# An order between the dense stream and the mixers, and a new allotment of dense work to each mixer step

## The chip, the cores and the metric

The kernel runs on one core of a Trainium2 chip. The metric is the device time of one execution in microseconds (us). Before the change three executions took 3931.73, 3942.15 and 3942.74 us; the median is 3942.15 us. A profile was taken of one execution, which took 3931.44 us.

## The reference

One layer of a hybrid encoder, for a prompt of 2048 rows and a sample group of 8 streams with 16 new rows each (128 rows). Model width 1024, four mixers A, B, C, D with four heads of 64, feed-forward width 2816, all in f32:

```python
h = rms_norm(x, norm_mix_g) * (1 + sc1) + sh1
cols = h @ w_in                          # columns for A, B, C, D
oa = gdn_mixer(cols_A, ...)              # A: gated delta rule in chunks of 64, state carried from chunk to chunk
ob = stick_breaking_attend(qb, kb, vb)   # B: strictly causal
oc = forgetting_attend(qc, kc, vc, f)    # C: causal softmax with a forget bias
od = band_attend(qd, kd, vd, bias)       # D: own chunk and the 8 before it
mixed = concat([oa] + [rms_norm(o, mg[i]) for i, o in enumerate((ob, oc, od))])
x = x + ga1 * (mixed @ w_o)
h = rms_norm(x, norm_ffn_g) * (1 + sc2) + sh2
u = causal_depthwise_conv(h @ w_up, ffn_conv_w, state)   # width 3
a, b = split(u)
x = x + ga2 * ((silu(a) * b) @ w_down)
```

The sample rows go through the same layer with caches of 1024 past rows (512 for D) and a carried state for A and for both convolutions. All new caches and states are outputs too.

## The kernel before

**Two streams of work.** The program is traced from two Python generators. The *dense* stream does the matrix products with the large weights: first the projections `proj` for four parts of 512 prompt rows (part 0 with the 128 sample rows), then four feed-forward blocks `ffn0` to `ffn3`, one a part (block 3 with the sample rows), each with the product by `w_o` at its start, `w_up` with the convolution, and `w_down`. Each f32 operand is split into a high and a low half (`hh`/`hl`, `mh`/`ml`, `gh`/`gl`), and three products with the halves (high by high, low by high, high by low) make one f32 product. The weights come through rings of tiles (`wu`, `wd`) that are loaded from a copy in DRAM. Between two feed-forward blocks stands a changeover: the next part's rows of `mixed` (the mixers' results, which went to DRAM) and of x are loaded to tiles `raw` and turned on PE, and the finished sums `acc` are turned and stored.

The *mixer* stream runs, part by part: for part 0, B, then A as `local0` (all of A that needs no state) and `steps0` (the recurrence), then C and D; for part 1, B1, C1, D1, then the sample rows of B (`sB`) side by side with `local1` and then `steps1`; for parts 2 and 3, the sample rows of C (D) side by side with `local2`, `steps2` (`local3`, `steps3`), then B, C and D of that part. `attn_prompt` writes a part's result of B, C or D with stores `mixed<-nsq` (line 874), and loads its operands from DRAM at the head of each phase: `qT` (line 902), the bias `add` (911), `kT` (997) and `vhl` (1004).

**What sets the order.** `weave` (line 133) alternates between the two. It takes one step of the mixers, under a priority so much higher (offset 100000) that the scheduler, which lays out each engine's instruction order ahead of time, places a mixer's instruction as soon as it takes it to be ready; each mixer step yields a number, its *pace*, which is added to a debt, and then dense steps are taken until the debt is paid (each says what it is worth). The pace comes from `lab` (line 167), which looks the phase's name up in the table `PACE` by its first two letters, then by its first. So `B2` and `C3` have entries of their own, `D` stands for D0 to D3, `lo` for local0 to local3, `st` for steps0 to steps3, and `s` for the sample phases. A phase with a low pace leaves dense work for later. Where the two streams depend on each other they yield a mark in place of a number: `mixers` waits for `proj0` to `proj3`, a feed-forward block for the mark `mix0` to `mix3` of its part. When the mixers are through, the dense stream goes on alone: this is most of `ffn3`.

`Order.step` (line 91) is taken around each step of either stream. It keeps the last PE instruction of every mixer step in the list `mix`. A dense step whose list `mix` is longer than `lag` gets an order dependency for its first PE instruction, on the last one of the mixer step `lag + 1` entries back. The dependency is one for the scheduler only (NoSync: both are on PE, no semaphore comes of it). `LAG` is 1000 (line 2131).

**PSUM.** Four pools of banks: `d` (3) for the dense products and turns, `z` (2), `ptr` (2) and `oT` (1) for the mixers. All matmuls are issued on line 89 and all transposes on line 92, so the tile's name tells what an instruction is: `d` for the dense stream, `z`, `ptr`, `oT` for the mixers.

Of the kernel before, what the change touches and what calls it, by code (L numbers as in the profile page):

```python
# [16 lines left out]
D = 1024  # L17
# [58 lines left out]
class Order:  # L76
# [17 lines left out]
    def step(self, g, dense, lag):  # L94


        self.now = []
        self.K.small = self.K.smalls[int(dense)]
        try:
            return next(g)  # L100
        finally:
            if not dense:
                if self.now:
                    self.mix.append(self.now[-1])
            elif self.now and len(self.mix) > lag:
                self.tc.add_manual_dep(self.now[0].ins, self.mix[-1 - lag].ins.name,
                                       mybir.DependencyInfo(mybir.DependencyClass.NoSync, mybir.DependencyReason.DATA), reason="order")
            self.now = None
# [17 lines left out]
def weave(K, dense, mixers, ahead, lag):  # L126

    debt, block = 0.0, None  # L130
    live = True

    def run_dense():
        nonlocal block, live
        try:
            c = K.pe.step(dense, True, lag)
        except StopIteration:
            live = False
            return 0.0
        block = c if isinstance(c, str) else None  # L140
        return 0.0 if block else c

    while True:
        try:
            with K.tc.high_priority(offset=ahead):
                c = K.pe.step(mixers, False, lag)
        except StopIteration:
            break
        if isinstance(c, str):
            while c not in K.done:  # L150
                run_dense()
                assert live and (block is None or block in K.done)
            continue
        debt += c
        while debt > 0 and live and (block is None or block in K.done):
            debt -= run_dense()
        debt = min(debt, 0.0)
    while live:
        run_dense()
# [6 lines left out]

def lab(nc, name, g):

    pace = PACE.get(name[:2], PACE.get(name[:1]))
    num = lambda: int(nc.get_next_instruction_name().split("-")[1]) if DEBUG else 0  # L170
    k = 0
    while True:
        a = num()
        try:
            c = next(g)
        except StopIteration as e:
            if DEBUG:
                MARKS.append((a, num(), name))
                print("phase", name, "steps", k)
            return e.value  # L180
        k += 1
        if DEBUG:
            MARKS.append((a, num(), name))
        yield pace * PHI if pace and not isinstance(c, str) else c


PACE = {"ga": 0.3, "B0": 0.9, "B1": 1.1, "B2": 0.8, "B3": 0.65, "C0": 0.8, "C1": 0.75, "C2": 0.6, "C3": 0.6, "D": 0.8, "lo": 0.6, "st": 0.6, "s": 0.4}


def chain(*gens):  # L190
    for g in gens:
        yield from g
# [232 lines left out]
def proj_stage(K, parts):  # L425
    yield from lab(K.nc, "proj", proj_parts(K, parts))
# [1051 lines left out]
def attn_samples(K, g, beside):  # L1478

    A = Ctx()  # L1480
    A.ev, A.wb, A.pb, A.sb = Eng(K.nc, 0.5), 2, 2, 1
    A.psum = lambda: K.mps("ptr")
    A.w = lambda m: A.sp.tile([P, P], F32, name="wn", bufs=1) if m <= P else A.sp.tile([P, 512], F32, name="w", bufs=A.wb)
    with K.tc.tile_pool(name="s" + g, bufs=1, side="right", reuse_waits="tile") as A.sp:
        yield from merge((lab(K.nc, "s" + g, samples_steps(K, A, g)), 1.0), (beside, 1.0))
# [260 lines left out]
def feed_stage(K):  # L1746

    tc = K.tc
    F = [Feed(K, p) for p in range(4)]
    yield "mix0"  # L1750
    copies = [(c, b) for c in "kv" for b in range(NB)]
    with ExitStack() as last:
        with tc.tile_pool(name="ff", bufs=2, side="left", reuse_waits="tile") as sp:
            for p in range(3):
                if p == 0:
                    rows = [sp.tile([P, 512], F32, name="acc", bufs=KT) for _ in range(KT)]
                    mod_columns(K, sp, rows)
                    yield from F[0].mixed(sp, raws(sp, F[0]))
                    yield from F[0].residual(0, sp, raws(sp, F[0]))
                    yield from F[0].residual(1, sp, raws(sp, F[0]))  # L1760
                if p < 2:
                    sa = lambda: sp
                else:
                    sa = lambda: last.enter_context(tc.tile_pool(name="fa", bufs=2, side="right", reuse_waits="tile"))
                sa = yield from lab(K.nc, f"ffn{p}", feed_block(K, F[p], sp, sp, F[p + 1], sa, copies))
        with tc.tile_pool(name="ff3", bufs=2, side="left", reuse_waits="tile") as sp:
            yield from lab(K.nc, "ffn3", feed_block(K, F[3], sa, sp, None, None, copies))
# [260 lines left out]
def mixers(K, G, p):  # L2028


    nc, O, I = K.nc, K.O, K.I
    beside = lambda g, n, q: merge((g, n), (lab(nc, f"gates{q}", gates(K, q)), 15))
    B = lab(nc, f"B{p}", attn_prompt(K, "B", p))
    local = lab(nc, f"local{p}", G.local_all(p))
    rest = lambda: chain(*[lab(nc, f"{g}{p}", attn_prompt(K, g, p)) for g in "CD"])
    if p < 3:
        local = beside(local, 50, (0, 2, 3)[p])
    rule = chain(local, lab(nc, f"steps{p}", G.steps_all(p)))

    def samples():  # L2040
        yield "proj3"
        if p == 3:
            nc.sync.dma_start(out=O["gdn_conv_p"], in_=K.a_pre[SEQ - 3:SEQ, 0:768])
        G.beside(True)
        yield from attn_samples(K, "BCD"[p - 1], rule)
        G.beside(False)

    yield f"proj{p}"
    if p == 0:
        yield from B  # L2050
        nc.sync.dma_start(out=O["gdn_conv_s"], in_=K.a_pre[SEQ:].rearrange("(b s) c -> b s c", s=16)[:, 13:16, 0:768])
        for _ in chain(gate_stage(K, NP, NT), gate_stage(K, 0, 4)):
            pass
        yield from rule
        yield from rest()
    elif p == 1:
        yield from beside(B, 79, 1)
        yield from rest()
        yield from samples()
    else:  # L2060
        yield from samples()
        yield from B
        yield from rest()
    K.done.add(f"mix{p}")


def trunk(tc, I, O):
# [3 lines left out]
    with ExitStack() as st:  # L2071
# [38 lines left out]
        dense = chain(proj_stage(K, parts), feed_stage(K))  # L2110
        K.pe.step(dense, True, LAG)
        with tc.issue_after(K.anchor.ins):
            load_consts(K, cp)
        gate_tiles(K, cp)
        G = Gdn(K, cp)
        weave(K, dense, chain(*[mixers(K, G, p) for p in range(4)]), 100000, LAG)

# [10 lines left out]


NF = 22  # L2130
LAG = 1000
OUTS = [
    ("y_p", (SEQ, D), (1, SEQ, D)), ("y_s", (P, D), (NB, 16, D)),
    ("gdn_conv_p", (3, 768), (1, 1, 3, 768)), ("gdn_state_p", (4, 64, 64), (1, 1, 4, 64, 64)),
# [26 lines left out]
```

## Time and profile before

| | before |
|---|---|
| runs, median (lowest to highest) | 3942.15 us (3931.73 to 3942.74) |
| profiled execution | 3931.44 us, span 3929.7 us |
| mean granted clock of TensorE | 0.961 |
| PE busy | 3660.0 us (93%), 22763 instructions |
| weight loads busy (beside PE) | 3162.0 us (80%) |
| VectorE (DVE) busy | 2437.6 us (62%) |
| ScalarE (ACT) busy | 1536.7 us (39%) |
| GpSimd (POOL) busy | 1431.8 us (36%) |
| HBM | 213 GB/s over the span |

An engine's busy time is the union of its instructions; PE's overlap, so a busy PE is not one at its peak, and the printed duration of a matmul is longer than the distance from one start to the next. The granted clock is the share of the full TensorE clock that the throttle allows. A window's row gives, for each engine, busy time and number of instructions, then the clock, the share of time in which the 16 DMA engines move data, and GB/s. In waits, `z L89 <- DMA kT<-kTD` reads: an instruction of line 89 that writes `z` waited for the transfer into `kT`.

### The profile page before, as it was taken

Reading aid. Unit: us, or ns where it says so; the run is one execution under the profiler, and the core shown is the slowest. Engines: PE = TensorE matmul, PEld = TensorE weight load, DVE = VectorE, ACT = ScalarE, POOL = GpSimd, SP = SyncE. Lnnn points to the kernel's source line nnn. Section 1 sums busy time; section 2 is a strip of 40 time slices with the busy share of each in tenths; the row PEclk is TensorE's granted clock in tenths of the full one; section 3 lists DMA queues with packets and bytes.
Section 4 is the critical chain, followed back from the end, with each engine's and each line's share of the span. In section 5 each row is a group of like instructions: output and inputs, shape, how many; then the busy total and the mean of one; then the engine's idle time right before and its main releaser. Section 6 shows DMA issues by size and latency. Waiting matters only on the chain. (4 is left out here: it accounts for less than half of the span.)

```text
span 3929.7 us, 66233 instructions
## 1 busy us (share of the span) xinstructions
PE 3660.0 (93%) x22763; PEld 3162.0 (80%) x22763; DVE 2437.6 (62%) x5592; ACT 1536.7 (39%) x3353; POOL 1431.8 (36%) x3487
## 2 busy tenths in 40 slices
PE   6998999999998999998999999689999996899999
PEld 4987889989986677775888788468787875899999
DVE  5668655464567785775487566765776665344444
ACT  4455323353355533542254344323553444232121
POOL 4456244362434434441465112333553112121121
PEclk7999999999999999998999999899999997999999
DMA  7887968777687888887454646564544633544442
GB/s 226 285 279 242 305 205 296 274 268 250 227 267 239 295 292 289 286 291 237 150 195 144 224 156 210 166 195 164 190 146 164 180 121 123 202 141 142 152 142 93
DMA packets 529077, 830.37 MB, mean 211 GB/s; under 512 B 112651, under 2 KB 351259, under 8 KB 528476
## 3 DMA queue, kind: packets, MB, share of 16 engines
q1 hardware_dynamic: 527269, 825.16, 63.4%
q8 instruction: 181, 2.97, 0.3%
q0 software_dynamic: 1472, 0.97, 0.1%
q14 instruction: 155, 1.27, 0.1%
HBM read 611.81 MB, written 224.16 MB: 213 GB/s over the span
## 5 line engine op out<-in xcount | busy, mean ns | idle before, releaser
L89 PE MATMUL d<-hh,wu 128*128 128x512 f32 (+1 forms) x3520 | 1016.8, 365 | 6.7 <-DMA wu<-keptw_up 4.5
L89 PEld LDWEIGHTS d<-hh,wu 128*128 128x128 f32 x3520 | 633.0, 190 | 98.7 <-issue 8.5
L89 PE MATMUL d<-w,hh 128*128 128x256 f32 (+2 forms) x3536 | 684.6, 289 | 26.3 <-DVE w L458 9.3
L89 PE MATMUL d<-hl,wu 128*128 128x512 f32 (+1 forms) x1760 | 639.3, 363 | 0.9 <-DVE hl L1862 0.7
L89 PEld LDWEIGHTS d<-w,hh 128*128 128x128 f32 x3536 | 562.2, 193 | 44.2 <-DVE w L458 11.6
L89 PE MATMUL d<-gh,wd 128*128 128x512 f32 (+1 forms) x1760 | 530.9, 370 | 13.0 <-DVE acc L1822 10.4
L89 PE MATMUL d<-w,hl 128*128 128x256 f32 (+2 forms) x1768 | 504.7, 287 | 0.2 <-DVE hl L407 0.2
L1912 DVE SCALAR_TENSOR_TENSOR cv<-u,fcw,cv 128x512 f32<-128x512 f32 (+1 forms) x440 | 299.9, 704 | 185.8 <-ACT cv L1910 177.7
L1822 DVE SCALAR_TENSOR_TENSOR acc<-d,mod,acc 128x512 f32<-128x512 f32 (+2 forms) x432 | 280.4, 655 | 187.7 <-PE d L89 187.1
L89 PEld LDWEIGHTS d<-gh,wd 128*128 128x128 f32 x1760 | 319.5, 190 | 67.2 <-DVE acc L1822 18.2
L89 PEld LDWEIGHTS d<-hl,wu 128*128 128x128 f32 x1760 | 333.3, 189 | 45.4 <-issue 3.7
L89 PEld LDWEIGHTS d<-w,hl 128*128 128x128 f32 x1768 | 338.8, 192 | 4.8 <-issue 3.3
L89 PE MATMUL d<-gl,wd 128*128 128x512 f32 (+1 forms) x880 | 319.7, 363 | 1.0 <-DVE gl L1974 1.0
L89 PE MATMUL z<-kT,qT 128*128 128x512 f32 (+3 forms) x864 | 261.2, 390 | 32.0 <-DVE mx L772 15.3
L839 ACT CAST wh<-ptr 128x512 fp32r<-128x512 f32 (+1 forms) x372 | 198.3, 552 | 208.6 <-PE ptr L92 116.8
L840 DVE TENSOR_TENSOR wl<-ptr,wh 128x512 fp32r<-128x512 f32 (+1 forms) x372 | 232.6, 639 | 74.7 <-ACT wh L839 68.7
L1899 ACT COPY u<-d 128x512 f32<-128x512 f32 (+1 forms) x220 | 110.3, 502 | 414.4 <-PE d L89 404.7
L740 DVE TENSOR_TENSOR_SCAN pr<-sn,pr,zeros 128x512 f32<-128x512 f32 (+3 forms) x172 | 223.8, 1308 | 31.4 <-ACT sn L732 24.6
L92 PE MATMUL ptr<-ident,w 128*128 128x128 f32 x1448 | 228.7, 278 | 13.5 <-POOL w L742 5.6
L1914 POOL COPY hal<-u 128x2 f32<-128x2 f32 x176 | 47.7, 271 | 523.2 <-ACT u L1899 520.9
L742 POOL TENSOR_TENSOR w<-w,pr 128x512 f32<-128x512 f32 (+3 forms) x168 | 187.6, 1119 | 114.2 <-DVE pr L740 61.2
L789 ACT ACTIVATE w<-w,nm 128x512 f32<-128x512 f32 (+3 forms) x284 | 174.2, 616 | 107.8 <-DVE nm L782 84.8
(610 smaller groups left out, 7175.1 us busy)
## 6 DMA issues: line engine op xcount, KB each, us to landing
wu<-keptw_up SPq DMA_DIRECT2D x264, 512.0 KB
w<-win SPq DMA_DIRECT2D x132, 512.0 KB
wd<-keptw_down SPq DMA_DIRECT2D x132, 512.0 KB
keptw_up<-wu SPq DMA_DIRECT2D x88, 512.0 KB
wu<-keptw_o SPq DMA_DIRECT2D x48, 512.0 KB
win<-w SPq DMA_DIRECT2D x44, 512.0 KB
raw<-in_w_up_dram SPq DMA_DIRECT2D x88, 256.0 KB
keptw_down<-wd SPq DMA_DIRECT2D x44, 512.0 KB
```

The costliest lines, as they stand in the source:

```text
L89: return self.note(self.nc.tensor.matmul(out, lhsT, rhs, **k))
L92: return self.note(self.nc.tensor.transpose(*a, **k))
L740: nc.vector.tensor_tensor_scan(out=pr[:, 0:m][:, ::-1], data0=sn[:, :m][:, ::-1], data1=K.zeros[:r, :m], initial=carry, op0=ALU.mult, op1= ...
L742: nc.gpsimd.tensor_tensor(w[:, :m], w[:, :m], pr[:, 1:m + 1], op=ALU.mult)
L789: self.K.nc.scalar.activation(w, w, AF.Exp, bias=self.nm, accum_out=self.l[:, s:s + 1])
L839: nc.scalar.copy(wh[:, c0:c1], pt[:, c0:c1])
L840: nc.vector.tensor_tensor(wl[:, c0:c1], pt[:, c0:c1], f(wh[:, c0:c1]), op=ALU.subtract)
L1822: nc.vector.scalar_tensor_tensor(acc[k][:, c0:m], ps[:, :m - c0], gate[:, k, 0:1], acc[k][:, c0:m], op0=ALU.mult, op1=ALU.add)
L1899: nc.scalar.copy(u[:, 2 + c0:2 + m], ps[:, :m - c0])
L1912: nc.vector.scalar_tensor_tensor(o, tap(i), cw[:, i:i + 1], o, op0=ALU.mult, op1=ALU.add)
L1914: nc.gpsimd.tensor_copy(K.hal[:, fi], tail)
```

## The change

Two things change. First, the order dependency holds only for dense steps that are traced after the projections' end (`proj3`) and before the mixers' end (`mix3`), and `LAG` is 12: there the first PE instruction of a dense step comes no earlier in PE's order than the last one of the mixer step 13 entries back. Second, the table of paces: a full name such as `local0` is looked up first, and the paces of B2, B3, C2, C3, D2, D3, of local1 to local3, steps1 to steps3 and of the sample phases are higher (D0, D1, local0 and steps0 keep theirs).

```diff
@@ Order.step
-            elif self.now and len(self.mix) > lag:
+            elif self.now and len(self.mix) > lag and "proj3" in self.K.done and "mix3" not in self.K.done:
                 self.tc.add_manual_dep(self.now[0].ins, self.mix[-1 - lag].ins.name,
@@ lab
-    pace = PACE.get(name[:2], PACE.get(name[:1]))
+    pace = PACE.get(name, PACE.get(name[:2], PACE.get(name[:1])))
...
-PACE = {"ga": 0.3, "B0": 0.9, "B1": 1.1, "B2": 0.8, "B3": 0.65, "C0": 0.8, "C1": 0.75, "C2": 0.6, "C3": 0.6, "D": 0.8, "lo": 0.6, "st": 0.6, "s": 0.4}
+PACE = {"ga": 0.3, "B0": 0.9, "B1": 1.1, "B2": 1.0, "B3": 0.83, "C0": 0.8, "C1": 0.75, "C2": 0.75, "C3": 0.75, "D0": 0.8, "D1": 0.8, "D": 0.9,
+        "local0": 0.6, "steps0": 0.6, "lo": 1.35, "st": 1.35, "s": 0.9}
...
-LAG = 1000
+LAG = 12
```

Both kernels have the same PE instructions; their order differs from the 4938th row of PE's on. Where the dense work stands is counted here, in PE's order, from the first mixer matmul of a phase to the first of the next (products of 512 columns or less into `d`, plus transposes into `d`; "others" are the mixers' own PE instructions). The times are those at which these first matmuls start in the trace of before, and the last row's time ends with the span's last products.

| phase | time before, us | dense before | others | dense after |
|---|---|---|---|---|
| D1 | 1085 to 1198 | 273 + 109 | 272 | 149 + 109 |
| sB, local1 | 1198 to 1464 | 727 + 0 | 513 | 594 + 0 |
| steps1 | 1464 to 1541 | 192 + 0 | 247 | 185 + 0 |
| sC, local2 | 1541 to 1852 | 736 + 96 | 673 | 884 + 0 |
| steps2 | 1852 to 1980 | 401 + 0 | 304 | 161 + 96 |
| B2 | 1980 to 2188 | 598 + 0 | 488 | 522 + 0 |
| C2 | 2188 to 2392 | 575 + 0 | 488 | 575 + 0 |
| D2 | 2392 to 2485 | 139 + 16 | 272 | 397 + 0 |
| sD, local3 | 2485 to 2637 | 250 + 80 | 376 | 360 + 96 |
| steps3 | 2637 to 2764 | 386 + 0 | 304 | 330 + 0 |
| B3 | 2764 to 3037 | 707 + 0 | 648 | 708 + 0 |
| C3 | 3037 to 3269 | 451 + 0 | 648 | 486 + 0 |
| D3 | 3269 to 3319 | 0 | 272 | 126 + 32 |
| changeover to ffn3 | 3319 to 3365 | 42 + 112 | 0 | 0 + 80 |
| ffn3 | 3365 to 3930 | 3576 + 40 | 88 | 3576 + 40 |

The order of PE's instructions at three places, as the scheduler left it. A row gives the line, the operation, out<-in, the tile's shape and how often it repeats. First, PE in steps2, before the change: a small product of the recurrence (`z<-Z,lT`, `oT<-kbv,lA`) among dense ones.

```order
L89 MATMUL d<-hh,wu 128x512 x2
L89 MATMUL z<-Z,lT 128x128 x4
L89 MATMUL d<-hl,wu 128x512
L89 MATMUL d<-hh,wu 128x512
L89 MATMUL d<-hl,wu 128x512
L89 MATMUL d<-hh,wu 128x512 x3
L89 MATMUL d<-hl,wu 128x512
L89 MATMUL d<-hh,wu 128x512 x2
L89 MATMUL d<-hl,wu 128x512
L89 MATMUL d<-hh,wu 128x512 x2
L89 MATMUL oT<-kbv,lA 128x64 x4
```

After the change the same pair of products, and those behind it, stand so:

```order
L89 MATMUL z<-Z,lT 128x128 x4
L89 MATMUL oT<-kbv,lA 128x64 x4
L92 MATMUL d<-ident,acc 128x128 x12
L89 MATMUL z<-lT,Z 128x128 x4
L89 MATMUL oT<-vn,kbv 128x128 x2
L89 MATMUL z<-S,gqet 128x128
L89 MATMUL z<-vn,lQ 128x64 x2
L89 MATMUL z<-S,gqet 128x128
L89 MATMUL z<-vn,lQ 128x64 x2
L92 MATMUL d<-ident,acc 128x128 x4
L89 MATMUL oT<-lA,lN 64x64 x4
```

Dense products stood between two dependent products of the recurrence; now there are fewer, and part of them are the transposes of `acc`, of the changeover from ffn0 to ffn1, which stood in local2 before.

Second, PE from C3 (its last rows are `oT<-wh,vhl` and the turn `oT<-j_676,os`) to D3 (whose scores are `z<-kT,qT`), before:

```order
L89 MATMUL oT<-wh,vhl 128x256
L89 MATMUL oT<-wl,vhl 128x256
L89 MATMUL oT<-j_676,os 128x64 x2
L89 MATMUL z<-kT,qT 128x512 x2
L89 MATMUL z<-kT,qT 128x384 x2
L89 MATMUL z<-kT,qT 128x128 x2
L89 MATMUL z<-kT,qT 128x256 x4
L89 MATMUL z<-kT,qT 128x128 x2
```

and after:

```order
L89 MATMUL d<-gh,wd 128x512 x2
L89 MATMUL d<-gl,wd 128x512
L89 MATMUL d<-gh,wd 128x512
L89 MATMUL oT<-j_676,os 128x64 x2
L89 MATMUL z<-kT,qT 128x512 x2
L89 MATMUL z<-kT,qT 128x384 x2
L89 MATMUL d<-gh,wd 128x512
L89 MATMUL d<-gl,wd 128x512
L89 MATMUL d<-gh,wd 128x512 x2
```

Dense products now stand ahead of C3's last turn and behind D3's second pair of scores, and none between the turn and the first scores, as before.

Third, SyncE's queue at the same place, which issues the stores and loads in its order, before:

```order
L874 DMA mixed<-nsq 128x4x64
L866 DMA hg<-in_merge_g_dram 128x64
L874 DMA mixed<-nsq 128x4x64
L902 DMA qT<-qTD 128x1024
L911 DMA add<-skew 128x640
L997 DMA kT<-kTD 128x512 x2
```

and after, where every line of the file is one further down:

```order
L875 DMA mixed<-nsq 128x4x64
L867 DMA hg<-in_merge_g_dram 128x64
L1801 DMA wu<-keptw_up 128x1024 x6
L875 DMA mixed<-nsq 128x4x64
L903 DMA qT<-qTD 128x1024
L912 DMA add<-skew 128x640
L998 DMA kT<-kTD 128x512 x2
```

Six loads of the dense stream's weights now stand ahead of C3's last store; D3's loads follow that store in both.

## Prediction

> **What bounds the kernel now.** I read the page's slices first, then the busy time of each stage, then the same stages with the tile `d` alone, and last the waits of the thin stages. The dense stream writes all its products to the PSUM tile `d`, the mixers write theirs to `z`, `ptr` and `oT`, so the count of `d` says how much dense work stands in a stage.
>
> ```profile
> PE   6998999999998999998999999689999996899999
> PEclk7999999999999999998999999899999997999999
> ```
>
> PE is at nine tenths or more nearly everywhere, so what can be won lies in a few slices: the head, which this change doesn't touch, the slices 25 and 26 (2456 to 2652 us) and 33 to 35 (about 3240 to 3440 us). First the price of a matmul where nothing waits: starts that follow each other in a run of dense products (start, us, what, count), a run of transposes, and a run of mixer products.
>
> ```profile
> 2599.66 0.62 PE L89 MATMUL d<-mh,wu 128*128 128x512 f32 x2
> 2600.12 0.39 PE L89 MATMUL d<-ml,wu 128*128 128x512 f32 x1
> 2600.34 0.62 PE L89 MATMUL d<-mh,wu 128*128 128x512 f32 x2
> ...
> 2448.01 0.71 PE L92 MATMUL d<-ident,raw 128*128 128x128 f32 x5
> 2448.55 0.49 PE L92 MATMUL ptr<-ident,w 128*128 128x128 f32 x3
> ```
>
> Three dense products start within 0.68 us, which makes 0.227 us each; five transposes take 0.54 us, 0.109 us each. The printed durations (0.62) overlap, so I do not use them. Now the stages: time, PE busy and count, PEld, DVE, ACT, POOL, granted clock, DMA share, GB/s.
>
> ```profile
> 1852.00:1980.00 128.00, 125.41 (x706) 103.53 (x706) 56.70 (x111) 33.08 (x61) 45.91 (x94) 1.00 0.51 172
> 1980.00:2188.00 208.00, 204.76 (x1090) 171.97 (x1089) 158.58 (x207) 101.76 (x204) 120.07 (x206) 1.00 0.49 167
> 2188.00:2392.00 204.00, 199.84 (x1063) 167.58 (x1062) 124.36 (x324) 87.00 (x193) 36.12 (x116) 0.99 0.58 190
> 2392.00:2485.00 93.00, 71.44 (x430) 61.27 (x428) 60.72 (x221) 40.65 (x109) 26.46 (x106) 0.94 0.48 156
> 2485.00:2637.00 152.00, 127.74 (x706) 90.24 (x706) 114.74 (x317) 47.48 (x119) 44.36 (x132) 0.92 0.67 212
> 3224.00:3269.00 45.00, 26.83 (x175) 22.29 (x173) 24.26 (x65) 18.34 (x43) 10.61 (x40) 0.81 0.18 51
> 3269.00:3319.00 50.00, 44.63 (x272) 37.90 (x272) 39.32 (x185) 30.02 (x92) 16.76 (x78) 0.89 0.40 132
> 3319.00:3365.00 46.00, 28.03 (x156) 22.24 (x155) 21.41 (x48) 12.92 (x34) 4.01 (x16) 0.81 0.57 181
> 3365.00:3930.00 565.00, 555.14 (x3704) 539.57 (x3704) 243.33 (x593) 132.25 (x310) 115.73 (x296) 0.99 0.43 143
> ```
>
> The same stages, and those between them, for the tile `d` alone (PE busy and count, clock, DMA):
>
> ```profile
> 1085.00:1198.00 113.00, 71.61 (x385) 0.95 0.81 260
> 1198.00:1464.00 266.00, 183.21 (x726) 0.96 0.83 274
> 1464.00:1541.00 77.00, 49.90 (x195) 1.00 0.89 296
> 1541.00:1852.00 311.00, 206.98 (x831) 0.95 0.84 277
> 1852.00:1980.00 128.00, 95.70 (x402) 1.00 0.51 172
> 1980.00:2188.00 208.00, 150.10 (x601) 1.00 0.49 167
> 2188.00:2392.00 204.00, 147.08 (x575) 0.99 0.58 190
> 2392.00:2485.00 93.00, 38.48 (x158) 0.94 0.48 156
> 2485.00:2637.00 152.00, 69.64 (x330) 0.92 0.67 212
> 2637.00:2764.00 127.00, 94.02 (x384) 0.97 0.53 176
> 2764.00:3037.00 273.00, 183.62 (x708) 0.97 0.46 152
> 3037.00:3224.00 187.00, 121.12 (x447) 0.96 0.57 174
> 3224.00:3269.00 45.00, 2.43 (x7) 0.81 0.18 51
> 3269.00:3319.00 50.00, 0.00 (x0) 0.89 0.40 132
> ```
>
> A stage with enough dense work is bound by PE's throughput. In B2 (1980 to 2188 us) 601 dense products at 0.227 us are 136 us, which leaves 72 us for the 489 others, 0.147 us each. C2 at the same prices needs 575 x 0.227 + 488 x 0.147 = 202 us, and took 204. A thin stage is longer than that: D2 (2392 to 2485) needs 33 us of dense work (139 products and 16 transposes) and 272 x 0.147 = 40, so 73 of its 93 us; the end of C3 (3224 to 3269) 27 of 45; D3 (3269 to 3319) 40 of 50. What PE waits for there, longest waits of these windows (total, times, longest):
>
> ```profile
> PE z L92 <- DMA gn<-apre: 15.4, 1, 15.4
> ...
> PE z L89 <- DMA kT<-kTD: 14.0, 1, 14.0
> ...
> PE d L92 <- DMA raw<-mixed: 12.3, 1, 12.3
> ```
>
> Three times the next mixer phase (or, the last time, the dense stream) waits for a load that stands behind a store of the phase before it, and no dense product is left to fill the time.
>
> **The change, part by part.** The added order is one of the scheduler alone: no semaphore, no instruction, no byte is added, and both kernels have the same matmuls. So the sum is over places: in each stage, the dense work that leaves or comes, at 0.227 us a product and 0.109 us a transpose, and how much of it is time there. The counts after are those of the table in the part on the change.
>
> Stages that give work away. D1 loses 124 products (28 us), sB with local1 133 (30 us), steps1 7 (2 us), steps2 240 products for 96 transposes (43 us), B2 76 (17 us), steps3 56 (13 us): 133 us together. Were PE always the bound there, all of it would be time. The granted clock is 0.95 to 1.00 in these rows and the dense counts leave little idle, so I take most of it. The other bound is that the mixers' own chains set the pace and nothing is saved: D3, with no dense work at all, took 50 us for the 272 products that D1 has too, and D1 would still have 46 us of dense work beside them. I take 27, 29, 2, 33, 16 and 13, in sum **-120**. Steps2 is cut most, because the changeover from ffn0 to ffn1 (96 transposes, each behind a load) moves into it.
>
> Stages that take work. sC with local2 gains 148 products and loses those 96 transposes: 23 us more, of which the changeover's idle time gives 3 back: **+20**. D2 gains 258 products for 16 transposes, 57 us. Its 20 idle us take some: 88 of the rows now stand between D2's last product and local3's first, which is 20 us against the 15.4 us wait for `gn`. So **+38**, between +37 (all idle time filled) and +57 (none). sD with local3 gains 27 us; of its 152 us the clock of 0.92 and the waits leave some 22 idle (330 dense and 376 others need 130), so it takes **+11**, between +5 and +27. C2 and B3 keep their counts: 0.
>
> The end of C3 and D3. C3 gains 35 products (8 us), and its last 45 us, that had 7 products, now have dense work throughout. But the longest wait there stays:
>
> ```profile
> 3254.71 0.66 PE L89 MATMUL oT<-j,os 128*128 128x64 f32 x4 [0.52 <-DVE os L71]
> 3269.38 1.83 PE L89 MATMUL z<-kT,qT 128*128 128x512 f32 x4 [14.01 <-DMA kT<-kTD]
> ...
> 3262.34 0.37 SPq L874 DMA_DIRECT2D mixed<-nsq  x1
> ...
> 3263.85 0.84 SPq L997 DMA_DIRECT2D kT<-kTD  x2
> ```
>
> SP issues C3's last store of `mixed` 7.6 us after PE's last product, the `kT` load behind it, and the load takes the rest. In the new order that store still stands ahead of that load, and still no dense row stands between the two products on PE, so 14 us remain. C3 as a whole asked 454 x 0.227 = 103 us for its dense products and 648 x 0.147 = 95 for the others, 198 of its 232 us, so 34 were idle or at a low clock; less the 14, of the other 20 the new work takes 15: 8 - 15 = **-7** (between +8, nothing filled, and -12, all of it). D3 gains 126 products and 32 transposes, 32 us, on 10 idle us: **+25**, between +22 and +32. Behind D3 the 12.3 us wait for `raw<-mixed` stays, but 42 products and 32 transposes (13 us) are gone from the stretch up to 3365 us; 80 transposes are left, which must follow 20 loads. **-12**, between 0 and -16. The last 565 us, ffn3 alone, do not change.
>
> The sum: -120 + 20 + 38 + 11 - 7 + 25 - 12 = -45 us on an execution of 3931.4 us (a span of 3929.7 and 1.7 around it): 3886. That execution stands at the lower end of the runs shown; their median is 10.7 us above it. A median may lie anywhere in that gap, so I add half, 5: **3891 us**.
>
> Loads: the weights' ring and their transfers are the same, and DMA's share is 0.89 at most in the rows above, so I price them at nothing; what hides them is the dense products of the group before. Where those stand closer together, in D2, a load that is late would cost its landing, up to the 5 us between issue and start that the `kT` rows show.
>
> The row that bears on the clock: 0.81 at the end of C3 and behind D3, 0.94 and 0.92 in D2 and local3, against 1.00 in B2. The Trainium skill, TensorE: Matmul & The Clock Gate, section "What's actually happening", says that PE falls to half its clock after an idle window of some 3.4 us and comes back after a busy one; the rows agree, as the low clocks stand with the waits of 12 to 15 us. By that rule the filled stages would run at the full clock too, which the sum above counts only in part; the result of it is the second rival below.
>
> **The rivals.** First, nothing is won: the thin stages are held by VectorE or by loads, and the work that they take is all time. D2, local3 and D3 would then cost 57 + 27 + 32 = 116 us in place of 74: -45 + 42 = -3, and with the 5 the time is 3933. Against it: VectorE was busy 60.7 of 93 and 39.3 of 50 us there, and dense work asks 243.3 us of it in the 565 us of ffn3, 0.43 a us, so D3 would have 53 us in 75. For it: the waits for `kT` and `raw` stay.
>
> Second, more is won: the clock. At 0.93 over the 245 us from 2392 to 2637, 34 us ran at half clock, and at 0.84 over the 141 us from 3224 to 3365, 45 us. If all that came back, half of it, 39 us, would be won beside the sum: 3891 - 39 = 3852. Against it: two of the three long waits stay, and part of the half clock lay in waits, where it costs nothing.
>
> Third, slower: in the early stages, D1 to B2 and steps3, the mixers' chains and not PE set the pace once the dense products between are thinned, and the dense work that was to be there comes later at full price. steps2 is the place: it has 161 products left of 401, and each of its small groups waits for ScalarE's or VectorE's copy of the one before. At worst none of the 120 us returns: 3891 + 120 = 4011. It decides the sign from the point where less than 75 of the 120 us are saved. Against it: D3 with no cover at all lost only 10 us on 272 products.
>
> Fourth, the change does not do what it says: the order would leave the mixers where they were. The new order on PE shows the counts moved, so I give that nothing.
>
> **How the numbers follow.** Forecast (3860 to 3915 us) 0.56; nothing won (3915 to 3945) 0.18; the clock (below 3860) 0.13; slower (above 3945) 0.13. The measurement can tell 0.3%, 12 us, from no change. Faster by more than that, below 3930: the forecast, the clock and nearly half of the second, 0.76; within it 0.14; slower, above 3954, 0.10. The range leaves out the upper end of the slow case and the lower end of the clock's: 3840 to 3945.
>
> **What would show it.** The stages by mixer phase: steps2 near 95 us, B2 near 190, D2 near 131, D3 near 75, and ffn3 unchanged. The wait for `gn` gone, those for `kT` and `raw` still at 14 and 12 us. If steps2 and D1 keep 128 and 113 us, the third case holds; if D2 takes 150, the first.

## The result and the profile after

| | before | after |
|---|---|---|
| median (lowest to highest) | 3936.99 us (3931.73 to 3942.74, 4 runs) | 3895.30 us (3889.05 to 3900.48, 4 runs) |
| ratio to before | | 0.9896, 95% interval 0.9878 to 0.9915 |
| profiled execution, span | 3931.44, 3929.7 us | 3892.44, 3890.7 us |
| mean granted clock | 0.961 | 0.967 |
| PE busy | 3660.0 us (93%) | 3628.3 us (93%) |

The change makes the kernel 1.0% faster, 39 us between the two profiled executions; the forecast was 45. The slices of the page of after, to be read against those of before:

```profile
PE   6998899989988999999999999989999987899999
PEclk7999999999998999999999999999999998899999
```

The hole at D2 and local3 (a 6 and an 8, 2456 to 2652 us) has become a single 8 (2529 to 2626 us, local3); from C3's end on, a 6 and an 8 have become an 8, a 7 and an 8. By stage, each from the first mixer matmul of a phase to the next one's (time, PE busy and count, PEld, DVE, ACT, POOL, clock, DMA share, GB/s):

```profile
1085.00:1180.00 95.00, 83.25 (x538) 72.91 (x537) 65.18 (x251) 51.71 (x140) 32.00 (x122) 0.89 0.70 224
1180.00:1423.00 243.00, 220.47 (x1121) 159.34 (x1122) 192.36 (x398) 118.03 (x222) 103.13 (x189) 0.94 0.82 265
...
1492.00:1806.00 314.00, 302.50 (x1583) 223.18 (x1582) 236.99 (x511) 138.01 (x277) 129.34 (x248) 0.99 0.86 287
1806.00:1900.00 94.00, 85.84 (x568) 73.24 (x569) 48.41 (x99) 29.79 (x70) 35.09 (x91) 0.95 0.70 238
...
2301.00:2430.00 129.00, 127.70 (x675) 108.71 (x674) 83.42 (x250) 50.56 (x123) 32.80 (x121) 0.99 0.57 185
2430.00:2611.00 181.00, 159.04 (x832) 116.12 (x830) 123.72 (x334) 58.34 (x138) 49.58 (x145) 0.92 0.65 212
...
2721.00:2986.00 265.00, 254.43 (x1358) 214.96 (x1356) 201.39 (x256) 131.75 (x261) 137.28 (x246) 0.98 0.50 161
...
3297.00:3328.00 31.00, 16.46 (x87) 12.78 (x88) 13.15 (x36) 10.13 (x29) 3.70 (x14) 0.64 0.80 276
```

D2 (2301 to 2430) is now full, 127.70 of 129 us, at a clock of 0.99 where it had 0.94. D1 (the first row) and steps2 (1806 to 1900) are shorter and worse used than before: D1 at a clock of 0.89 where it had 0.95, steps2 busy for 91% at 0.95 where it was busy for 98% at 1.00. Local3 (2430 to 2611) is longer and idles still, and B3 (2721 to 2986) is shorter with the same dense work. The long waits, from local3's start (start, us, what, count) and from the end of C3 on (total, times, longest):

```profile
2429.54 0.39 PE L89 MATMUL d<-hh,wu 128*128 128x512 f32 x1
2429.77 0.38 PE L92 MATMUL z<-ident,gn 128*128 128x128 f32 x2
```

```profile
PE ptr L92 <- DMA stn<-in_state_ffn_conv_dram: 18.3, 2, 9.6
PE z L89 <- DMA kT<-kTD: 13.8, 1, 13.8
PE d L92 <- DMA raw<-mixed: 4.1, 2, 3.0
```

The wait for `gn` (15.4 us) is gone: a dense product runs until local3's first turn. That for `kT` is as it was. Behind D3, 18.3 us are now put down to loads of `stn` (rows of the sample's convolution state) that the new order places ahead of the turns of `raw`. D3's last turn starts at 3287.1 us and ffn3's first product at 3327.5, so the stretch between is 40 us long (47 before); the last row of the stages above begins after the first wait for `stn`.

The lengths of all stages, from the starts in the trace (D3 with the changeover behind it, since the border between the two moved), with what was forecast. The last two columns are the change once more in another execution, and the new paces without the order ("paces alone" from here on), both from experiments below.

| stage | before | after | difference | forecast | after, again | paces alone |
|---|---|---|---|---|---|---|
| head, to D1 | 1085.1 | 1085.4 | +0.3 | 0 | 1087 | 1093.3 |
| D1 | 112.9 | 94.1 | -18.8 | -27 | 94.0 | 110.4 |
| sB, local1 | 266.5 | 243.2 | -23.3 | -29 | 244.5 | 261.0 |
| steps1 | 76.9 | 69.6 | -7.3 | -2 | 68.8 | 75.2 |
| sC, local2 | 310.9 | 313.6 | +2.7 | +20 | 312.9 | 301.0 |
| steps2 | 128.1 | 94.5 | -33.6 | -33 | 98.2 | 127.6 |
| B2 | 207.5 | 198.7 | -8.8 | -16 | 199.8 | 210.1 |
| C2 | 204.4 | 202.3 | -2.1 | 0 | 204.1 | 204.1 |
| D2 | 92.9 | 128.5 | +35.6 | +38 | 128.8 | 94.8 |
| sD, local3 | 152.1 | 181.3 | +29.2 | +11 | 181.3 | 160.8 |
| steps3 | 127.1 | 110.1 | -17.0 | -13 | 110.1 | 137.2 |
| B3 | 273.0 | 265.2 | -7.8 | 0 | 264.2 | 253.7 |
| C3 | 231.9 | 228.6 | -3.3 | -7 | 228.7 | 226.3 |
| D3 and changeover | 96.1 | 112.4 | +16.3 | +13 | 111.0 | 77.9 |
| ffn3 | 559.5 | 558.2 | -1.3 | 0 | 558.3 | 558.2 |

### The profile page after: what moved, and what is told of

Read it like the earlier page. It is cut to its first block, busy times and chain, and to the rows that moved or that the text cites. A ratio compares the mean times of both kernels' runs of the same rounds, so it can differ in the third digit from the quotient of the medians.

```text
span 3890.7 us, 66224 instructions
## 1 busy us (share of the span) xinstructions
PE 3628.3 (93%) x22763; PEld 3147.3 (81%) x22763; DVE 2437.3 (63%) x5592; ACT 1537.0 (40%) x3352; POOL 1406.7 (36%) x3487
## 4 chain that ended last, share of the span: by engine, by line
PE 62%; DMA 11%; DVE 9%; POOL 4%; issue 3%; ACT 2%; SPq 1%; POOLq 0%; DVEq 0%; ACTq 0%
PE d L89 44%; PE z L89 5%; PE oT L89 5%; PE ptr L92 4%; PE ptr L89 2%; PE d L92 1%; DVE pr L741 1%; DMA w<-win 1%; DMA add<-nF 1%; DVE gy L1184 1%; DVE cv L1913 1%; DMA wraw<-in_ada_w_dram 1%; DMA raw<-in_x_prompt_dram 1%; PE z L92 1%; DVE acc L1823 1%
## 5 line engine op out<-in xcount | busy, mean ns | idle before, releaser
L89 PE MATMUL z<-kT,qT 128*128 128x512 f32 (+3 forms) x864 | 255.8, 385 | 34.7 <-DMA kT<-kTD 13.8
L741 DVE TENSOR_TENSOR_SCAN pr<-sn,pr,zeros 128x512 f32<-128x512 f32 (+3 forms) x172 | 217.8, 1275 | 24.3 <-ACT sn L733 18.8
```

What stands on the lines that cost most here:

```text
L89: return self.note(self.nc.tensor.matmul(out, lhsT, rhs, **k))
L741: nc.vector.tensor_tensor_scan(out=pr[:, 0:m][:, ::-1], data0=sn[:, :m][:, ::-1], data1=K.zeros[:r, :m], initial=carry, op0=ALU.mult, op1= ...
```

## The experiments

**The two parts apart.** First the order with the old paces (the lookup by full name changes nothing there):

```diff
-PACE = {... "B2": 1.0, "B3": 0.83, ... "C2": 0.75, "C3": 0.75, "D0": 0.8, "D1": 0.8, "D": 0.9,
-        "local0": 0.6, "steps0": 0.6, "lo": 1.35, "st": 1.35, "s": 0.9}
+PACE = {... "B2": 0.8, "B3": 0.65, ... "C2": 0.6, "C3": 0.6, "D": 0.8, "lo": 0.6, "st": 0.6, "s": 0.4}
```

> The order (12 steps back) with the paces of before. In PE's order it takes too much dense work out of the mixers' stages: 1794 more products than before stand in the last stage, ffn3 alone (407 us at 0.227 us). My theory, that a thinned stage gives its work's price back only as long as the mixers' own chains leave room: most stages fall to those chains, and the kernel is slower than before, 3960 to 4050 us. Rival, the order alone makes the gain and the paces matter little: 3880 to 3905 us, since the work on PE is the same.

Measured: 4156.85 us, ratio 1.0565 (1.0521 to 1.0610). Slower, as the theory said, and by more than it said. Its windows of steps2 and B2:

```profile
1717.00:1805.00 88.00, 66.13 (x419) 54.56 (x419) 36.45 (x69) 23.15 (x47) 38.87 (x86) 0.87 0.52 166
1805.00:2006.00 201.00, 164.71 (x867) 135.88 (x868) 158.37 (x196) 101.04 (x209) 123.37 (x198) 0.92 0.50 163
```

steps2 has 47 products and 96 turns fewer than in the change (21 us) and is 7 us shorter. B2 has 378 dense products here, 144 fewer than in the change (33 us), and takes 201 us against 199: nothing of that work's price comes back. PE idles for 36 of its 201 us, at a clock of 0.92. The longest waits in it:

```profile
PE z L89 <- DMA kT<-kTC: 15.9, 1, 15.9
PE ptr L92 <- DVE wl L840: 7.2, 6, 3.2
PE oT L89 <- ACT oh L73: 5.7, 3, 3.5
```

So the mixers' own chain (VectorE's and ScalarE's work between two products) is only part of it. The longest wait is for C2's first load, at B2's end, which in the change dense products cover almost whole. From D1 to C3 this run waits six times so at a phase's head for `kT`, 93 us together; the change does it for 20 us.

Then the paces without the order:

```diff
-LAG = 12
+LAG = 1000
```

> The new paces without the order (1000 steps back). The dense counts of the stages are those of before, at most 58 products off in one stage (steps3). My theory, that paces alone don't hold dense work back because the scheduler pulls it ahead wherever a mixer instruction isn't ready: the time of before within 0.4%, 3920 to 3950 us. Rival, the higher paces are the gain: under 3910 us.

Measured: 3902.79 us, ratio 0.9911 (0.9879 to 0.9943). My theory fell. The dense counts by stage are those of before, and yet most of the gain is there. So both were run again beside each other:

> The changed kernel once more, unaltered, beside the paces alone on the same chip: 3885 to 3905 us. Its profile shows how far a stage's length differs from execution to execution; I expect under 4 us for each stage but the head.

> The paces without the order once more, unaltered, for the difference to the changed kernel on the same chip. Theory, the order adds something to the paces (it fills D2, D3 and local3, which idle without it): 5 to 15 us slower than the changed kernel. Rival, the order gives and takes the same (it fills three stages and thins five): within 3 us of it. By stages I expect B3 again some 20 us shorter than before the change; if it is 265 us or more, that reading of the first run was chance.

Measured: the change 3899.72 us, ratio 0.9910 (0.9895 to 0.9926); the paces alone 3895.91 us, 0.9903 (0.9889 to 0.9916). The two medians stand 3.8 us apart, the paces alone the faster, and the intervals overlap: not the theory, and the rival within the noise. **The order gives and takes the same.** Stages repeat within 4 us (the table), and B3 took 253.8 us in the first run of the paces alone, so its 253.7 us are not chance either. The windows of D2, local3, B3 and of D3 with the changeover, paces alone:

```profile
2382.00:2477.00 95.00, 73.26 (x431) 62.69 (x429) 61.06 (x221) 40.69 (x109) 26.60 (x106) 0.91 0.46 153
2477.00:2638.00 161.00, 130.62 (x708) 92.67 (x708) 113.62 (x327) 49.16 (x122) 44.54 (x133) 0.89 0.65 207
2775.00:3029.00 254.00, 248.77 (x1351) 211.47 (x1349) 204.99 (x255) 129.99 (x259) 149.00 (x245) 1.00 0.49 163
...
3255.00:3333.00 78.00, 56.98 (x353) 47.12 (x354) 52.12 (x220) 39.68 (x119) 20.61 (x92) 0.85 0.49 158
```

D2 and local3 idle as before the change; B3 doesn't. B3 has 699 dense products here and had 707: 2 us less work, 19 us less time. PE idles for 5 of its 254 us and the clock is full throughout; before the change it idled for 13 of 273 us and ran 17 us at half clock. B3's window before the change, and what PE waited for in it:

```profile
2764.00:3037.00 273.00, 259.81 (x1356) 217.02 (x1355) 207.01 (x255) 130.97 (x260) 151.39 (x245) 0.97 0.46 152
```

```profile
PE d L89 <- DVE acc L1822: 6.4, 5, 2.8
PE ptr L92 <- DVE wl L840: 2.6, 4, 1.1
```

A dense product waits five times because its bank of `d` isn't free: VectorE has not yet added the earlier product to `acc`. With the paces alone no such wait is left in B3. From the start times in the trace, the sum into `acc` begins on VectorE 3.5 us after the last product of its group has begun in B3 before the change (mean of 40 groups), 2.2 us with the paces alone (39), and 3.2 us in the change (40). The earlier start alone is not the cause: with half of the table (the run of local, steps and the sample phases without the order, below) it is 3.3 us, five such waits still make 3.7 us, and the clock stays full. One of the waits, before the change, and what follows it on PE:

```profile
2983.72 0.80 PE L89 MATMUL d<-gh,wd 128*128 128x512 f32 x1 [2.77 <-DVE acc L1822]
2984.31 0.63 PE L89 MATMUL d<-gl,wd 128*128 128x512 f32 x1
2984.74 1.05 PE L89 MATMUL d<-gh,wd 128*128 128x512 f32 x2
2985.59 0.63 PE L89 MATMUL d<-gl,wd 128*128 128x512 f32 x1
...
2988.58 0.63 PE L89 MATMUL d<-gh,wd 128*128 128x512 f32 x1
2989.00 0.41 PE L89 MATMUL oT<-wh,vhl 128*128 128x256 f32 x1
```

Three products now start within 1.28 us where they took 0.68. From 2983.72 to 2989.00 there are twelve, 5.3 us in place of 2.7. So a wait of 2.8 us stands with a loss of 5.3.

**The paces in parts.** With the order, the new paces of local, steps and the sample phases only:

```diff
- ... "B2": 1.0, "B3": 0.83, ... "C2": 0.75, "C3": 0.75, "D0": 0.8, "D1": 0.8, "D": 0.9,
+ ... "B2": 0.8, "B3": 0.65, ... "C2": 0.6, "C3": 0.6, "D": 0.8,
```

> The order, with only the new paces of local, steps and the sample phases; B2, B3, C2, C3, D2, D3 keep those of before. Up to C2 the counts are those of the change. B3 and C3 have 144 and 90 products fewer (53 us), D2 109 fewer, D3 132 more, and 282 products with 112 turns are left for the stretch behind D3, which in the change has 80 turns and idles some 20 us. My theory, that a stage gives its price as long as work is left in it, and that idle time is where the dense work runs out: 3870 to 3890 us, the stretch behind D3 some 80 us long without a wait over 5 us for raw or stn. Rival, the thinner B3 and C3 are held by the mixers' chains: 3895 to 3920 us.

Measured: 3958.21 us, ratio 1.0054 (1.0037 to 1.0070). Slower than before the change; theory and rival both put it too fast. C2, B3 and the stretch behind D3:

```profile
2108.00:2305.00 197.00, 177.39 (x968) 148.80 (x969) 117.56 (x314) 83.63 (x188) 35.73 (x113) 0.96 0.55 176
2728.00:2984.00 256.00, 225.57 (x1213) 190.03 (x1213) 189.95 (x237) 123.06 (x250) 147.63 (x236) 0.94 0.45 148
...
3298.00:3392.00 94.00, 83.60 (x394) 66.13 (x394) 50.52 (x88) 26.98 (x57) 14.69 (x35) 0.96 0.53 179
```

C2 has 95 products fewer than in the change (22 us) and is 5 us shorter, B3 144 fewer (33 us) and 9 us shorter. With 564 products B3 takes 256 us, with 699 (paces alone) 254. B3's longest wait:

```profile
PE z L89 <- DMA kT<-kTC: 19.1, 1, 19.1
```

It is 19 of the 30 us that PE idles in B3, so the rival's chains are the smaller part: thinning uncovered the load at the head of C3 (and 16.4 us for D2's `kT` at C2's end). Behind D3 the left-over work does cover the wait (83.60 of 94 us busy), but it had been taken from stages that then idled.

Then those of B, C and D only:

```diff
- "local0": 0.6, "steps0": 0.6, "lo": 1.35, "st": 1.35, "s": 0.9
+ "lo": 0.6, "st": 0.6, "s": 0.4
```

> The order, with only the new paces of B2, B3, C2, C3, D2, D3; local, steps and the sample phases keep those of before (0.6, 0.6 and 0.4). local2, steps2 and steps3 are thin (470, 126 and 120 products), and 1696 more products than in the change stand in ffn3 alone. My theory: slower than the change by 20 to 100 us, 3915 to 3990 us, the loss in sB, sC, sD and the steps. Rival, only the paces of B, C and D matter: 3880 to 3905 us.

Measured: 4120.83 us, ratio 1.0468 (1.0434 to 1.0502). In the direction of the theory, and again more than it said; so the new paces of B, C and D do not carry the order by themselves.

Without the order, the same two halves, local, steps and the sample phases first:

```diff
- ... "B2": 1.0, "B3": 0.83, ... "C2": 0.75, "C3": 0.75, "D0": 0.8, "D1": 0.8, "D": 0.9,
+ ... "B2": 0.8, "B3": 0.65, ... "C2": 0.6, "C3": 0.6, "D": 0.8,
...
-LAG = 12
+LAG = 1000
```

> No order (1000 steps back); new paces for local, steps and the sample phases alone. The dense counts up to D2 are within 13 products of before; local3 has 86 more, B3 48 more, C3 144 fewer. If the gain of the paces comes from the stages that these paces belong to (sB, sC, steps), it is 10 to 25 us here (3910 to 3925 us) and sC is some 8 to 10 us shorter than before. Rival: the gain comes from B3 and C3's own paces, and this is within 8 us of before (3927 to 3943 us).

And B, C and D:

```diff
- "local0": 0.6, "steps0": 0.6, "lo": 1.35, "st": 1.35, "s": 0.9
+ "lo": 0.6, "st": 0.6, "s": 0.4
...
-LAG = 12
+LAG = 1000
```

> The complement: no order, new paces for B2, B3, C2, C3, D2, D3 alone. If the gain comes from these, 3905 to 3920 us and B3 near 255 us in place of 273; if from the other half, within 8 us of before, and sB and sC as before. If the halves' gains add up, they make the 39 us of both; if neither gives more than 10 us, the gain hangs on the whole table, since the dense stream's lead is what both build up together.

Measured: 3916.44 us, ratio 0.9945 (0.9924 to 0.9966), and 3949.26 us, ratio 1.0022 (1.0008 to 1.0035). The first lies in its theory's range, and sC is 12.9 us shorter in it, where 8 to 10 were expected. The second is 9 us slower, outside both of its ranges. 24 us faster and 9 us slower don't make the 39 us of both. B3 in the two:

```profile
2780.00:3049.00 269.00, 263.28 (x1405) 221.93 (x1403) 202.74 (x258) 130.99 (x262) 147.49 (x247) 1.00 0.49 162
2817.00:3094.00 277.00, 265.62 (x1412) 223.13 (x1410) 206.84 (x260) 133.87 (x265) 147.14 (x251) 1.00 0.48 159
```

By its length B3 is short in neither, but it holds 755 and 763 dense products there, 48 and 56 more than before (11 and 13 us). For its work it is 15 and 8.5 us shorter, and the clock is full in both. So B3's gain does not need both halves. C3 has 144 and 169 products fewer (33 and 38 us) and is only 26 and 33 us shorter. Why the halves don't add up over the whole kernel is not shown.

**The waits that stayed.** The store of the last head of every C phase goes out from GpSimd, which computes it, and not from SyncE:

```diff
-def head_norm(K, A, gi, h, oh, nt, dst):
+def head_norm(K, A, gi, h, oh, nt, dst, queue=None):
...
-    nc.sync.dma_start(out=dst, in_=sq)
+    (queue or nc.sync).dma_start(out=dst, in_=sq)
...
-                head_norm(K, A, gi, H.h, H.oh, 4, K.mixed[r:r + 512, c:c + 64].rearrange("(t p) d -> p t d", p=P))
+                head_norm(K, A, gi, H.h, H.oh, 4, K.mixed[r:r + 512, c:c + 64].rearrange("(t p) d -> p t d", p=P),
+                          nc.gpsimd if g == "C" and H.h == 3 else None)
```

> The changed kernel with one store of each C phase (that of its last head) issued by GpSimd, which also computes it, in place of SyncE; so D's first loads no longer stand behind it on SyncE. Theory, the wait of D3's first scores for kT is made by that place in the queue: it falls from 13.8 us to 4 to 8 us, and the kernel gains 5 to 10 us (C0 to C2 end under dense work and gain nothing). Rival, the loads wait for the memory that C3's tiles leave, or GpSimd's issue costs as much: the wait stays above 11 us and the time within 4 us of the changed kernel.

Measured: 3888.24 us, ratio 0.9882 (0.9867 to 0.9897), beside 3899.72 for the unaltered change on the same chip: 11 us less, though the two intervals touch. SyncE's queue at C3's end, after and then here:

```profile
3208.84 0.37 SPq L875 DMA_DIRECT2D mixed<-nsq  x1
3209.30 0.46 SPq L903 DMA_DIRECT2D qT<-qTD  x1
...
3210.34 0.86 SPq L998 DMA_DIRECT2D kT<-kTD  x2
```

```profile
3191.20 13.54 SPq L1802 DMA_DIRECT2D wu<-keptw_up  x4
3204.83 0.38 SPq L903 DMA_DIRECT2D qT<-qTD  x1
...
3207.58 0.80 SPq L999 DMA_DIRECT2D kT<-kTD  x2
```

D3's loads no longer stand behind the store, and PE's wait for `kT` (13.8 us) is gone; C3 is 15 us shorter than in the change. What is late next is VectorE's maximum of the scores, and D3 is 6 us longer:

```profile
PE z L89 <- DVE mx L773: 6.5, 1, 6.5
```

Two buffers for the tile in which a head's squares and its result stand:

```diff
-    sq = A.sp.tile([P, nt, 64], F32, name="nsq", bufs=1)
+    sq = A.sp.tile([P, nt, 64], F32, name="nsq", bufs=A.nsq)
...
+    A.nsq = 2 if (g, part) in NSQ2 else 1
...
+NSQ2 = (("C", 2), ("D", 2), ("C", 3), ("D", 3))
```

> The changed kernel with two buffers for the tile nsq in C2, D2, C3 and D3, so that the squares of a head don't wait until the store of the head before has landed (8.8 us on GpSimd at the end of D3). Theory, that wait is on the path behind D3: the last store of mixed goes out 5 to 9 us earlier and the kernel gains 3 to 8 us, all in the stretch behind D3. Rival, the turns of stn, which stand ahead of those of raw on PE and wait for loads behind 4 MB of weights, take its place: within 2 us of the changed kernel.

Measured: 3899.47 us, ratio 0.9915 (0.9901 to 0.9929): no difference, as the rival had it. PE's waits behind C3 are those of the change:

```profile
PE ptr L92 <- DMA stn<-in_state_ffn_conv_dram: 18.1, 2, 10.2
PE z L89 <- DMA kT<-kTD: 13.7, 1, 13.7
PE d L92 <- DMA raw<-mixed: 3.8, 3, 2.9
```

Last, GpSimd's store for D0 to D2 too, first without the order (`LAG` 1000 in place of 12, as shown), then with it (`LAG` stays 12):

```diff
-                          nc.gpsimd if g == "C" and H.h == 3 else None)
+                          nc.gpsimd if (g == "C" or g == "D" and part < 3) and H.h == 3 else None)
...
-LAG = 12
+LAG = 1000
```

> The paces without the order, with the last store of each C phase and of D0 to D2 issued by GpSimd. It takes away two of the three long waits instead of filling them: kT ahead of D3 (13.1 us with the paces alone) and gn ahead of local3 (15.8 us), each down to 3 to 8 us. Theory: 15 to 20 us faster than the paces alone, 3876 to 3885 us. Rival: what the waits hid (other loads of the next phase behind the same queue, VectorE's first maxima) takes their place, as in D3 where the run with one store moved left 6.5 of 13.7 us: 3885 to 3893 us.

> The whole change (order and paces) with the same stores moved to GpSimd. Behind D2 its 88 dense rows cover the wait for gn already, so the second store should bring nothing beyond the 11 us that the first brought: 3884 to 3894 us. Rival: it brings another 5 us or more (under 3883 us), since a shorter wait leaves those rows for a later gap.

Measured: 3884.43 us, ratio 0.9857 (0.9838 to 0.9877), the fastest of all kernels run; and 3894.70 us, ratio 0.9889 (0.9872 to 0.9906), no better than with C's store alone, as the theory had it. The paces alone gain by it 11 us by the medians (3895.91 before) or 18 by the ratios to the kernel before on each chip (0.9903), so the run stands at the border of theory and rival. What PE waits for at D2's end and from C3's end on, paces alone with both stores moved:

```profile
PE z L92 <- DVE gy L1192: 9.7, 1, 9.7
PE z L92 <- DMA gn<-apre: 6.2, 1, 6.2
```

```profile
PE d L92 <- DMA raw<-mixed: 15.0, 1, 15.0
PE z L89 <- DVE mx L773: 9.1, 3, 8.4
```

The wait for `kT` is gone and that for `gn` is 6.2 us where it was 15.6, but VectorE's work behind those loads partly takes the place, and the wait for `raw` is about as long as it was (13.7 us). Moving the stores also changed where dense work stands (71 products more in D2, 70 fewer in sB with local1), so the gain is not the waits' alone.

## Why the prediction came out as it did

The time was forecast at 3891 us and measured at 3895.30; the sum was -45 us and the profile shows -39. Most of the terms fit their stages. The reason that I gave for them doesn't carry the gain.

**What held.** Six stages that give work away were put at -120 us and gave 108.8. D2 was put at +38 and took 35.6, with the wait for `gn` gone; D3 with the changeover at +13 and took 16.3; C3 at -7 and gave 3.3, with the wait for `kT` unchanged at 13.8 us. ffn3 is the same. The prices, 0.227 us a product and 0.109 a turn, put D2 at 131 us; it took 128.5.

**What was off in size.** sC with local2 took 2.7 us, not 20: the changeover that left it had cost far more there than the 3 us that I gave it (PE idle 25 us before and 11.5 after, clock 0.95 and 0.99), and in steps2 PE idles only 6 us more. sD with local3 took 29.2, not 11: it has the idle time of a changeover still (159.04 of 181 us busy), and no more of it was filled. The two errors, -17 and +18, cancel. Behind D3 the wait for `raw` was to stay at 12 us. It is 4.1 us, but 18.3 for `stn` stand ahead of it. The stretch from D3's last turn to ffn3 is 40 us long where the forecast came to 34; D3 itself took 72 us where I had 75, which hides part of that in the sum.

**Which step failed.** The total agreed, but not by the step that it rests on: "So the sum is over places: in each stage, the dense work that leaves or comes". The sum counted the paces only through the work that they and the order move. The runs show two effects instead. The paces alone, which move almost nothing between stages, are worth the whole gain (0.9903 against 0.9910). And the moved work is worth nothing: between the last two columns of the table, the order takes 695 products out of D1, sB, steps1, steps2, B2 and steps3 (with the paces alone they have 273, 729, 197, 388, 605 and 444) and puts 96 turns in, 147 us by the prices, and these stages are 106 us shorter; the same 147 us come to sC, D2, local3, B3, C3 and D3, which are 112 us longer. The fill hides 35 us, as forecast in kind; the thinning loses 41, where I allowed 13. "I take most of it" was the mis-sized term. PE's idle time shows the same: against the paces alone it grows by 32 us in the six stages that gave work away and falls by 32 in the six that took it. This is the third rival's effect inside the forecast, though not by the mixers' chains alone: in the thinned D1 and sB, PE waits for loads too (7.1 us for `ck`, the sample rows' cache, in sB). Against before it looked like 24 us (109 of 133): with the paces alone these six stages hold 59 products more than before (13 us) and are only 2.5 us longer.

So the total agreed by luck: a loss that I took too small met a gain that I had not seen.

**The rivals.** That nothing is won in the filled stages fell in D2, which took 36 of 57 us, and in D3, which took 23 of 32; in local3 it holds, 29 for 27 us of work. The clock came up in D2 (0.94 to 0.99) and sC (0.95 to 0.99) and went down in D1 (0.95 to 0.89) and steps2 (1.00 to 0.95); on the whole 0.961 to 0.967. From D1 on, 201 us at half clock became 178 (181 in the second execution): at most some 12 us, a part of the 39 and not a gain beyond the sum. The slower case did not come for the change as made, but the order with the old paces is it, in full (1.0565): the paces are what keeps the order from emptying the stages.

**What stays open.** How the paces alone win 39 us is traced in size, and by waits in B3 alone. From D1 on PE idles 177 us before the change and 161 with the paces alone, and the time at half clock falls from 201 to 164 us (184 in the first run of the paces alone). A us at half clock costs at most half a us, so that is 16 us of idle time and up to 19 us of clock. sC (10 us), D3 with the changeover (18 us, 13 of them work that stands elsewhere) and sB (5.5 us) are shorter as well as B3. Which step of the new order within a stage brings this was not traced. Nor was it why the two halves of the table don't add up.

## What to carry to other kernels

Filling idle time with work from elsewhere is a gain only by the difference of two prices: what the work costs where it comes (D2: 36 of 57 us) and what comes back where it leaves (here 106 of 147 us; in B2 nothing of 33 us, once the next phase's load and the mixers' own chain were left uncovered). Run the parts of such a change apart before believing a sum that fits: two wrong terms can make a right total. Where a wait at a phase's head is for a load queued behind a store, moving the store to another queue (11 us with one edit) is cheaper than bringing work to cover it.

## What the runs showed of the hardware

A wait on PE well under 3 us can cost as much again in clock. In the rows above, 2.77 us of waiting are followed by twelve products at nearly twice their distance (0.427 us in place of 0.227), 2.6 us more; the clock stood at half from 2982.60 to 2989.42 us. The Trainium skill, TensorE: Matmul & The Clock Gate, section "What's actually happening", gives windows of 3413 ns and the drop for an idle one. The low clock's length fits: in the trace it lasts 3.41 or 6.83 us in B3 before the change. That the window must be idle throughout does not. In the 3.41 us before this drop PE was busy for 44%, with the end of a product and eight turns; the wait had lasted 1.65 us by then.

The traces of this case say more. All drops of one trace lie on one grid of 3.413 us. Take the windows of that grid between D1 and ffn3 that ran at the full clock. Before the change there were 19 in which PE was busy for less than half (the union of its instructions), and all 19 were followed by half clock; of the 594 others five were. With the paces alone it is 13 of 14, and 3 of 596. The windows ahead of B3's three drops before the change were 47%, 48% and 44% busy. By these counts it is the sum of idle time in a window that goes with a drop, and not one long wait. So short waits that recur, five of them for one engine's sums, are worth looking for beside the long ones.
